# Two-layer mLSTM and neighbourhood-attention backbone on one core: finished mLSTM tiles transposed one projection later, a weight subtraction on GpSimd, and an end spread over four projections

## The chip, the cores and the metric

The kernel runs on one core of a Trainium2 chip. The metric is device time in microseconds (us) of one execution. A core has a matmul engine (TensorE, PE in the profile; its weight loads are PEld), three engines for elementwise work (VectorE or DVE, ScalarE or ACT, GpSimd or POOL), and SyncE (SP), which here issues the transfers (DMAs) between memory and the core. Each engine works through its own instructions in order; semaphores make one wait for another. Matmuls accumulate in PSUM banks, all other tiles lie in SBUF.

## The reference

Two layers on 1024 latent tokens and 256 context tokens of width 1024. In each layer one projection feeds two head groups, an mLSTM (a matrix memory, run in both directions over chunks of tokens) with 8 heads, and neighbourhood attention with 8 heads; their outputs are projected together, and a squared-ReLU MLP follows. Cut to the part in question:

```python
def step(carry, xs):                     # mlstm_scan, one chunk of tokens
    C, n, m = carry
    ...
    s = jnp.einsum('bhtd,bhsd->bhts', qc, kc) * w_intra
    num = w_prev[..., None] * jnp.einsum('bhtd,bhde->bhte', qc, C) + jnp.einsum('bhts,bhse->bhte', s, vc)
    qn = w_prev * jnp.einsum('bhtd,bhd->bht', qc, n) + jnp.sum(s, axis=-1)
    h = num / jnp.maximum(jnp.abs(qn), jnp.exp(-m_t))[..., None]
    ...
    C = w_c[..., None, None] * C + jnp.einsum('bhs,bhsd,bhse->bhde', w_s, kc, vc)
...
y = (head_layernorm(hx_f + hx_b, norm_g) * jax.nn.sigmoid(o.astype(f32))).astype(q.dtype)
...
y_m, yc_m = mlstm_group(qm, km, vm, om, gm, qmc, kmc, vmc, omc, gmc, b_gate, norm_g, cos, sin, need_ctx)
y_n, yc_n = neighborhood_attention(qn, kn, vn, qnc, knc, vnc, rpb, rows, need_ctx)
y = jnp.concatenate([y_m, y_n], axis=-1)
x = x + g1 * (y @ w_out[l])
```

In the last layer the mLSTM and attention outputs of the context tokens are not needed.

## The kernel before

Every large matmul is made of three (L94 to L96, `mm3`): each operand is split into a high part in a reduced format and a low part, and high times high, high times low and low times high are added up in one bank. For weights, `split_chunk` (from L74) loads a chunk of 128x1024 into one of two buffers `wraw`; ACT casts it to `whi` (L88), and DVE subtracts to get `wlo` (L89). There are four such pairs. For the chunks of the mLSTM projection `less_last` (L82) first subtracts, inside each head, the last value column from the other 63.

The mLSTM stage (`mlstm_kv`, then `mlstm_out`) goes over four pairs of heads (`pr`) and, inside a pair, over five slots `i` of 256 tokens. `project_j` makes a slot's projection: two banks of 24 matmuls each, 512 columns wide, or 256 in slots without an output tile (the context slot of the last layer). Four chunks of weights belong to a pair, so a new set is split at each pair boundary. Keys and values taken from a projection at pair `pr` are those of the next pair. A slot with an output gives a tile: queries `qr`, the output gate `og` (ACT, then a product on POOL, L657), and a decay table `w` that a DMA broadcasts (`w<-gscr`, L644) and DVE (L662) and ACT (L663) turn into weights.

Behind a projection stands a `gap`, which does three steps of the pipeline, for three different tiles:

- for the newest tile: transposes of the queries (L573), scores and the state's part (L673, L674), and on DVE the scores weighed (L682) and the state's part scaled (L691);
- for the tile before it: values (L699, out of bank by ACT as `nt`, L702), transposes back (L708), and the norm on DVE (`mlstm_norm`, L714 to L737), which divides, normalizes and multiplies by the gate, into a tile `hs` (two buffers, its constant column set by POOL, L723);
- for the tile before that: two transposes of `hs` (`mlstm_turn`, L747), ACT's copy `yT` (L750), and a store to memory (L752).

A gap also makes the transposes of new keys (L504) and the state updates: DVE scales values into `vw` (L521), PE multiplies them with the keys (L532), and DVE adds up the states (L539, L546). At the start of the stage this is done for all five slots of the first pair in one go, ten L521 and forty L532, with six `vw` buffers.

At the end of the stage the queries and keys of attention are begun: `qk_project(W, gi, ...)` for three groups of tokens `gi` (context 256, then 512 and 512), keys first. `mlstm_out` makes the three key projections, with the last two gaps between them, and `na_qk` then evicts the keys (L800 on ACT, L801 on DVE), makes the query projections and evicts them (L813, L814 on ACT, L816 on DVE). In attention L955 and L965 are the scores.

Pools with a number of buffers and a scheduler that fixes the order of each engine's instructions before the run decide where an instruction stands; `behind()` holds PE work behind the PE instruction that was written last. L158 and L183 belong to the opening (the modulation by `c`), L209 is a piece of the modulation of later steps that DVE does in between.

The lines that set the end of `mlstm_out` (L627 to L638):

```python
with self.behind():
    keys.append(self.qk_project(Wq[0], 0, hi, lo))
gap(due[len(seq)])
with self.behind():
    keys.append(self.qk_project(Wq[0], 1, hi, lo))
gap([])
keys.append(self.qk_project(Wq[0], 2, hi, lo, "q"))
self.mlstm_turn(l)
return Wq, keys
```

Of the kernel before, what the change touches and what calls it, by code (L numbers as in the profile page):

```python
# [11 lines left out]
F32 = mybir.dt.float32  # L12
# [11 lines left out]
HD = 64  # L24
# [23 lines left out]
class Kern:  # L48
# [30 lines left out]
    def less_last(self, raw, n, c):  # L79

        v = raw[:, :n].rearrange("p (k c) -> p k c", c=c)[:, :, 128:256].rearrange("p k (h e) -> p k h e", e=HD)
        self.nc.vector.tensor_sub(v[:, :, :, 0:HD - 1], v[:, :, :, 0:HD - 1], v[:, :, :, HD - 1:HD].to_broadcast([128, n // c, 2, HD - 1]))  # L82

    def split_raw(self, raw, n):
        nc = self.nc
# [424 lines left out]
    def kv_weigh(self, pr, i):  # L510
# [7 lines left out]
        for u in range(2):  # L518
            vw = self.mp.tile([128, 256], F32, name="vw", bufs=WV)[:].rearrange("p (s h e) -> p s h e", s=2, h=2)
            ws = tab[:, 2 * i + u, 1, :, pr * 2:pr * 2 + 2].unsqueeze(3).to_broadcast([128, 2, 2, 64])  # L520
# [36 lines left out]
    def mlstm_out(self, l, hi, lo, need_ctx, W):  # L557

        n2, skip = NT // 2, 0 if need_ctx else 1
        seq = [(pr, i) for pr in range(4) for i in range(n2)]  # L560
        groups = [[(pr, i) for i in range(o, min(o + GROUP, n2))] for pr in range(4) for o in range(skip, n2, GROUP)]
        due = {seq.index(g[-1]) + 1: g for g in groups}
        self.scored, self.turning, states, tiles = [], [], [], {}
        Wq, keys = [], []

        def gap(group):

            now = [tiles.pop(t) for t in group]
            with self.behind():
                p = self.bank() if now or states else None  # L570
                for z, t in enumerate(now):
                    for u in range(2):
                        self.nc.tensor.transpose(p[:, (2 * z + u) * 128:(2 * z + u + 1) * 128], t["qr"][:, u, :], self.ident)  # L573
                spare = 2 - len(now)
                held = [self.kv_turn(*s, p[:, (len(now) + z) * 256:(len(now) + z + 1) * 256]) for z, s in enumerate(states[:spare])]
                if now:
                    n = len(now) * 256
                    qT = self.mb.tile([128, 256 * GROUP], F32, name="qT", bufs=2)
                    self.nc.scalar.mul(qT[:, :n], p[:, :n], 0.125)
                    for z, t in enumerate(now):  # L580
                        t["qT"] = qT[:, z * 256:(z + 1) * 256].rearrange("p (u t) -> p u t", u=2)
                for f in held:
                    f()
                for s in states[spare:]:
                    self.kv_turn(*s)
                self.mlstm_turn(l)
            with self.behind():
                for s in states:
                    self.kv_state(*s)
                    if s[1] == n2 - 1:  # L590
                        self.kv_back(s[0])
                states.clear()
                for t in self.scored:
                    self.mlstm_values(t)
            with self.behind():
                for t in now:
                    self.mlstm_scores(t)
            with self.behind():
                for t in self.scored:
                    self.mlstm_back(t)  # L600
            for t in now:
                self.mlstm_weigh(t)
            for t in self.scored:
                self.mlstm_norm(t)
            for t in now:
                self.mlstm_before(t)
            self.scored = now
            self.tick(True)

        for n, (pr, i) in enumerate(seq):  # L610
# [3 lines left out]
            with self.behind():  # L614
                accs = self.project_j(W, i, hi, lo, 512 if mine else 256)
# [10 lines left out]
            if pr < 3:  # L626
                self.kv_weigh(pr + 1, i)  # L627
                states.append((pr + 1, i))
        Wq.extend(self.qk_weights(l, 0, which) for which in (1, 0))
        with self.behind():  # L630
            keys.append(self.qk_project(Wq[0], 0, hi, lo))
        gap(due[len(seq)])
        with self.behind():
            keys.append(self.qk_project(Wq[0], 1, hi, lo))
        gap([])
        keys.append(self.qk_project(Wq[0], 2, hi, lo, "q"))
        self.mlstm_turn(l)
        return Wq, keys  # L638

    def mlstm_tile(self, l, pr, i, acc):  # L640
        nc, mp = self.nc, self.mb
        tab = self.gt[0]
        w = mp.tile([128, 2, 2, 256], F32, name="w", bufs=GB)
        nc.sync.dma_start(w[:].rearrange("p s h t -> p (s h) t"),  # L644
# [65 lines left out]
    def mlstm_norm(self, t):  # L710

        nc, mp, tab, i, pr, hh = self.nc, self.mb, self.gt[0], t["i"], t["pr"], t["hh"]
# [6 lines left out]
        nc.vector.tensor_tensor(den[:], den[:], tab[:, 2 * i:2 * i + 2, 3, :, pr * 2:pr * 2 + 2], ALU.max)  # L719
        nc.vector.reciprocal(d8, d8)  # L720
        nc.vector.tensor_tensor(h8[:, :, 0:63], h8[:, :, 0:63], d8.unsqueeze(2).to_broadcast([128, 8, 63]), ALU.mult)
        hs = mp.tile([128, 2, 2, 64], F32, name="hs", bufs=2)
        nc.gpsimd.memset(hs[:, :, :, 63:64], 0.0)  # L723
        nc.vector.tensor_add(hs[:, :, :, 0:63], hh[:, :, 0, :, 0:63], hh[:, :, 1, :, 0:63])
        hs4 = hs[:].rearrange("p u h e -> p (u h) e")
# [9 lines left out]
            nc.vector.tensor_scalar(hs4[:, z, :], hs4[:, z, :], mv[:, z, 0:1], rs[:, z:z + 1], ALU.subtract, ALU.mult)  # L735
        hsf = hs[:].rearrange("p u h e -> p u (h e)")
        nc.vector.tensor_mul(hsf, hsf, t["og"][:])  # L737
        self.turning.append((pr, i, hsf))

    def mlstm_turn(self, l):  # L740

# [41 lines left out]
    def na_qk(self, l, pr, hi, lo, need_ctx, W=(), accs=()):  # L783
# [6 lines left out]
        for which in (1, 0):  # L790
            wh, wl = W[1 - which] if W else self.qk_weights(l, pr, which)
            for gi, (g0, n) in enumerate(GROUPS):
                if which == 0 and gi == 0 and not need_ctx:
                    continue
                acc = accs[gi] if which == 1 and gi < len(accs) else self.qk_project((wh, wl), gi, hi, lo)
                for h in range(2):
                    a, b = slice(h * 64, h * 64 + 64), slice(64 - h * 64, 128 - h * 64)
                    if which == 1:
# [1050 lines left out]
WRAW = 2  # L1849
VB = 10  # L1850
TB = 7
WV = 6
GROUP = 1
GB = 4
OB = 5
QB = 3
CONSTS = {"cT": 16, "ident": 128, "fg": 8, "n1g0": 8, "n2g0": 8, "n1g1": 8, "n2g1": 8, "bada0": 48, "bada1": 48, "bgate0": 2, "bgate1": 2}
# [120 lines left out]
```

## Time and profile before

| | |
|---|---|
| median of 3 runs | 2904.61 us (2904.39 to 2906.29) |
| the profiled execution | 2902.07 us |
| its span, first to last instruction | 2900.3 us |
| mean granted PE clock | 0.992 |
| busy: PE, DVE, ACT, POOL | 97%, 76%, 44%, 2% |
| the mLSTM stage's `mlstm_out`, layer 0 | about 125 to 456 us |
| the same, layer 1 | about 1681 to 1970 us |

A row of the timeline gives start and duration in us, engine, line, operation, out<-in, the tile's shape, and in brackets the idle time of that engine before it and what ended it. Rows of groups give count, busy time and mean in ns, and behind the bar the idle time before them. "PE q L747 <- DVE hs L737: 20.4, 8, 5.6" says that PE's L747 waited for DVE's L737 for 20.4 us in all, 8 times, 5.6 at most. Durations in a timeline overlap a little, since matmuls are pipelined; the distance between two starts is the better measure there.

### The profile page before, as it was taken

To read this page: it belongs to the slowest core of one execution; us is meant where nothing else is said; L and a number is where in the kernel's file an instruction comes from. 1 tells how busy PE (TensorE), PEld (TensorE's weight loads), DVE (VectorE), ACT (ScalarE), POOL (GpSimd) and SP (SyncE) were. 2 spreads that over 40 slices of the span, in tenths; PEclk is the share of its full clock that TensorE was granted. 3 is DMA by queue.
4 is the path that set the end of the run, shared out by engine and by line. 5 is a ranking of instruction groups with operands and counts; after the bars stand their busy time and mean duration, and the time that the engine had idled before them with its cause. 6 is when DMAs were issued, how large, how long until landed. Compare 5 with 4: busy or idle time off the path is not lost.

```text
span 2900.3 us, 45396 instructions
## 1 busy us (share of the span) xinstructions
PE 2825.2 (97%) x16500; PEld 2383.2 (82%) x16500; DVE 2205.7 (76%) x4947; ACT 1267.6 (44%) x2472; POOL 70.4 (2%) x153
## 2 busy tenths in 40 slices
PE   8999999999999999999999999999999999999998
PEld 5877778888888888888889987778887788888888
DVE  7779977776798777589877778767775887769774
ACT  5333334564553333344554333325564533334443
POOL 0000000010000000000000000000010000000000
PEclk9999999999999999999999999999999999999999
DMA  7434422236446555798977222223346354478672
GB/s 247 134 122 138 150 77 87 91 114 203 149 156 237 192 196 199 271 322 287 322 256 251 69 77 77 73 67 109 113 137 196 128 177 152 156 246 311 218 250 101
DMA packets 279264, 497.40 MB, mean 171 GB/s; under 512 B 23648, under 2 KB 119904, under 8 KB 279040
## 3 DMA queue, kind: packets, MB, share of 16 engines
q1 hardware_dynamic: 279040, 494.50, 51.1%
q8 instruction: 130, 2.13, 0.3%
q14 instruction: 94, 0.77, 0.1%
HBM read 398.82 MB, written 95.59 MB: 170 GB/s over the span
## 4 chain that ended last, share of the span: by engine, by line
PE 73%; DVE 12%; issue 6%; DMA 5%; ACT 2%; SPq 1%; DVEq 0%; POOL 0%; ACTq 0%; POOLq 0%
PE q L94 13%; PE q L96 13%; PE q L95 13%; PE mm L94 9%; PE mm L95 9%; PE mm L96 9%; PE q L1017 1%; DVE wlo L89 1%; PE q L699 1%; DMA raw<-hid 1%; DMA S<-rpbt 1%; PE q L673 1%; DMA w<-gscr 1%; PE q L965 1%; PE q L983 1%
## 5 line engine op out<-in xcount | busy, mean ns | idle before, releaser
L94 PE MATMUL q<-ah,whi 128*128 128x512 f32 (+1 forms) x1472 | 550.5, 374 | 3.1 <-ACT ah L1067 2.4
L96 PE MATMUL q<-ah,wlo 128*128 128x512 f32 (+1 forms) x1472 | 548.1, 372 | 0.7 <-DVE wlo L1068 0.5
L95 PE MATMUL q<-al,whi 128*128 128x512 f32 (+1 forms) x1472 | 548.7, 373 | 0.0
L94 PE MATMUL mm<-ah,whi 128*128 128x512 f32 (+1 forms) x1120 | 387.3, 346 | 1.5 <-ACT whi L88 1.2
L96 PE MATMUL mm<-ah,wlo 128*128 128x512 f32 (+1 forms) x1120 | 385.3, 344 | 0.5 <-DVE wlo L89 0.5
L95 PE MATMUL mm<-al,whi 128*128 128x512 f32 (+1 forms) x1120 | 385.5, 344 | 0.0
L94 PEld LDWEIGHTS q<-ah,whi 128*128 128x128 f32 x1472 | 278.1, 189 | 52.3 <-ACT ah L1067 3.4
L96 PEld LDWEIGHTS q<-ah,wlo 128*128 128x128 f32 x1472 | 277.8, 189 | 50.8 <-DVE wlo L1068 1.8
L95 PEld LDWEIGHTS q<-al,whi 128*128 128x128 f32 x1472 | 278.3, 189 | 49.1 <-issue 1.4
L94 PE MATMUL mm<-whi,ah 128*128 128x512 f32 (+2 forms) x864 | 311.6, 362 | 1.6 <-ACT whi L88 1.1
L95 PE MATMUL mm<-wlo,ah 128*128 128x512 f32 (+2 forms) x864 | 308.6, 358 | 3.0 <-DVE wlo L89 2.7
L96 PE MATMUL mm<-whi,al 128*128 128x512 f32 (+2 forms) x864 | 308.0, 357 | 0.0
L94 PEld LDWEIGHTS mm<-ah,whi 128*128 128x128 f32 x1120 | 212.4, 190 | 29.0 <-issue 2.0
L96 PEld LDWEIGHTS mm<-ah,wlo 128*128 128x128 f32 x1120 | 212.5, 190 | 26.2 <-DVE wlo L89 1.0
L95 PEld LDWEIGHTS mm<-al,whi 128*128 128x128 f32 x1120 | 212.6, 190 | 25.2 <-issue 0.2
L1067 ACT CAST ah<-raw 128x512 fp32r<-128x512 f32 (+1 forms) x264 | 142.9, 566 | 121.9 <-PE q L96 58.4
L95 PEld LDWEIGHTS mm<-wlo,ah 128*128 128x128 f32 x864 | 164.9, 191 | 26.8 <-DVE wlo L89 5.1
L94 PEld LDWEIGHTS mm<-whi,ah 128*128 128x128 f32 x864 | 164.3, 191 | 26.6 <-ACT whi L88 2.4
L96 PEld LDWEIGHTS mm<-whi,al 128*128 128x128 f32 x864 | 164.6, 191 | 22.8
L1068 DVE TENSOR_TENSOR al<-raw,ah 128x512 fp32r<-128x512 f32 (+1 forms) x264 | 158.0, 622 | 26.9 <-ACT ah L1067 26.7
L1068 DVE TENSOR_TENSOR wlo<-raw,whi 128x1024 fp32r<-128x1024 f32 x84 | 102.6, 1223 | 69.8 <-ACT whi L1067 67.3
L94 PE MATMUL q<-th,whi 128*128 128x512 f32 x384 | 150.3, 391 | 2.1 <-DVE s L1232 2.0
(292 smaller groups left out, 5216.1 us busy)
## 6 DMA issues: line engine op xcount, KB each, us to landing
raw<-w SPq DMA_DIRECT2D x168, 512.0 KB
raw<-hid SPq DMA_DIRECT2D x104, 512.0 KB
wada<-w_adaT SPq DMA_DIRECT2D x96, 512.0 KB
wraw<-w SPq DMA_DIRECT2D x80, 512.0 KB
hid<-hb SPq DMA_DIRECT2D x128, 256.0 KB
hid<-ht SPq DMA_DIRECT2D x96, 256.0 KB
w<-gscr SPq DMA_DIRECT2D x36, 512.0 KB
wada<-w_ada SPq DMA_DIRECT2D x32, 512.0 KB
```

Of the source, the lines that this page charges most:

```text
L89: nc.vector.tensor_sub(lo[:, :n], raw[:, :n], fview(hi[:, :n]))
L94: mm(out, lh, rh, start=start, stop=False, skip_group_check=True)
L95: mm(out, lh, rl, start=False, stop=False, skip_group_check=True)
L96: mm(out, ll, rh, start=False, stop=stop, skip_group_check=True)
L673: mm(t["S"][h][:, o:o + 128], st["kT"][i][hp, u, :], t["qT"][hp, u, :], start=True, stop=True, skip_group_check=True)
L699: self.nc.tensor.matmul(p[h * 64:(h + 1) * 64, u * 256:(u + 1) * 256].rearrange("p (s t) -> p s t", s=2), va[:, u, h, :], t["w"][:, :, h, ...
L965: mm(sl[:, :nl].rearrange("p (r w) -> p r w", w=Rw[1]), q[2 * h + z], krhs[h], start=z == 0, stop=z == 1)
L983: nc.tensor.transpose(tp[:, (h * 2 + a) * 128:(h * 2 + a + 1) * 128], Pn[h][:, a * 128:(a + 1) * 128], self.ident)
L1017: self.nc.tensor.matmul(yp[h * 64:(h + 1) * 64, :], v[h], pt[h], start=i == 0, stop=i == len(tiles) - 1, skip_group_check=True)
L1067: ins = self.nc.scalar.copy(hi, src)
L1068: self.nc.vector.tensor_sub(lo, src, fview(hi))
```

## The change

Four things. `less_last` runs on GpSimd. A normalized tile is put on a list `normal` first and moves to `turning` at the end of the next gap's transposes, so that it is transposed one gap later than before, with three `hs` buffers. The end of `mlstm_out` makes four projections, named by `(which, gi)` with 1 for keys and 0 for queries, and the last steps of the pipeline stand between them one by one; the query projection (0, 1) is among them and is left out of `na_qk`. And there are ten `vw` buffers instead of six, and three `w` buffers instead of four.

```diff
     def less_last(self, raw, n, c):
...
-        self.nc.vector.tensor_sub(v[:, :, :, 0:HD - 1], v[:, :, :, 0:HD - 1], v[:, :, :, HD - 1:HD].to_broadcast([128, n // c, 2, HD - 1]))
+        self.nc.gpsimd.tensor_sub(v[:, :, :, 0:HD - 1], v[:, :, :, 0:HD - 1], v[:, :, :, HD - 1:HD].to_broadcast([128, n // c, 2, HD - 1]))
...
-        self.scored, self.turning, states, tiles = [], [], [], {}
-        Wq, keys = [], []
+        self.scored, self.turning, self.normal, states, tiles = [], [], [], [], {}
+        Wq, keys = [], {}
...
                 self.mlstm_turn(l)
+                self.turning, self.normal = self.normal, []
...
+        def project(which, gi, tag="mm"):
+
+            with self.behind():
+                keys[which, gi] = self.qk_project(Wq[1 - which], gi, hi, lo, tag)
+
+        project(1, 0)
+        gap(due[len(seq)])
+        project(1, 1)
         with self.behind():
-            keys.append(self.qk_project(Wq[0], 0, hi, lo))
-        gap(due[len(seq)])
+            self.mlstm_turn(l)
+            for t in self.scored:
+                self.mlstm_values(t)
+        project(1, 2, "q")
+        self.turning, self.normal = self.normal, []
         with self.behind():
-            keys.append(self.qk_project(Wq[0], 1, hi, lo))
-        gap([])
-        keys.append(self.qk_project(Wq[0], 2, hi, lo, "q"))
+            for t in self.scored:
+                self.mlstm_back(t)
+            self.mlstm_turn(l)
+        for t in self.scored:
+            self.mlstm_norm(t)
+        project(0, 1, "q")
+        self.turning = self.normal
         self.mlstm_turn(l)
         return Wq, keys
...
-        hs = mp.tile([128, 2, 2, 64], F32, name="hs", bufs=2)
+        hs = mp.tile([128, 2, 2, 64], F32, name="hs", bufs=3)
...
-        self.turning.append((pr, i, hsf))
+        self.normal.append((pr, i, hsf))
...
-                acc = accs[gi] if which == 1 and gi < len(accs) else self.qk_project((wh, wl), gi, hi, lo)
+                acc = accs[which, gi] if (which, gi) in accs else self.qk_project((wh, wl), gi, hi, lo)
...
-WV = 6
+WV = 10
...
-GB = 4
+GB = 3
```

The changed file has 17 more lines from L628 on, so that a line of `mlstm_norm` or `mlstm_turn` has a number 17 higher there: L747 is L764, L737 is L754, L699 is L716, L955 is L972, L662 is L679, and the L708 of DVE in the new order is the L691 of before. The scheduler's order moves with the change. Three places, with the name of the semaphore's engine where an instruction waits.

PE at the end of layer 1's mLSTM, where attention begins. Before, nine of the matmuls of the next pair's key projection (L94 to L96) stand between the last query projection and the first scores (L955):

```order
L94 MATMUL mm<-ah_14589,whi 128x512 [waits DVE_49]
L95 MATMUL mm<-al_14597,whi 128x512
L96 MATMUL mm<-ah_14589,wlo 128x512
L94 MATMUL mm<-ah_14590,whi 128x512
L95 MATMUL mm<-al_14598,whi 128x512
L96 MATMUL mm<-ah_14590,wlo 128x512
L94 MATMUL mm<-ah_14591,whi 128x512
L95 MATMUL mm<-al_14599,whi 128x512
L96 MATMUL mm<-ah_14591,wlo 128x512
L955 MATMUL q<-nk_20651,nq 128x256 [waits DVE_49]
```

Now, from the end of the query projection (0, 1) on:

```order
L96 MATMUL q<-ah_15279,wlo 128x512
L764 MATMUL q<-consts,hs 128x128 [waits DVE_49,PE_49,Pool_49]
L764 MATMUL q<-consts,hs 128x128
L94 MATMUL mm<-ah_14589,whi 128x512 [waits DVE_49]
L95 MATMUL mm<-al_14597,whi 128x512
L96 MATMUL mm<-ah_14589,wlo 128x512
L94 MATMUL mm<-ah_14590,whi 128x512
L972 MATMUL q<-nk_20676,nq 128x256 [waits DVE_49]
```

The last transposes of `hs` have moved from ahead of the projection (0, 1) to behind it, and four matmuls are left between them and the first scores.

DVE at the second pair boundary of layer 0, where `wlo` of the first two weight chunks is made (L89), before:

```order
L521 TENSOR_TENSOR vw<-va,tab 128x256 [waits Pool_49]
L89 TENSOR_TENSOR wlo<-wraw,whi 128x1024 [waits Activation_49]
L447 TENSOR_TENSOR ropea<-mm,cos 128x128 [waits PE_49]
L447 TENSOR_TENSOR ropeb<-mm,sin 128x128
L89 TENSOR_TENSOR wlo<-wraw,whi 128x1024 [waits Activation_49]
L450 TENSOR_TENSOR kt<-ropea,ropeb 128x4x32 [waits DVE_49]
```

Now the first chunk stands where it stood, and the second here, behind the next tile's norm has begun (L731 to L738):

```order
L735 SCALAR_TENSOR_TENSOR den<-hh 128x8 [waits DVE_49]
L708 TENSOR_TENSOR hh<-q,tab 128x4x64
L736 TENSOR_TENSOR den<-den,tab 128x8 [waits DVE_49]
L209 ISA wada,mod<-wada,consts 128x1024 [waits DMAHW7_49]
L209 ISA mod 128x1
L737 RECIPROCAL den<-den 128x8 [waits DVE_49]
L89 TENSOR_TENSOR wlo<-wraw,whi 128x1024
L738 TENSOR_TENSOR hh<-hh,den 128x8x63 [waits DVE_49]
L89 TENSOR_TENSOR wlo<-wraw,whi 128x1024 [waits DMAHW0_49,Activation_49]
```

The second chunk's subtraction has moved behind a piece of modulation (L209), and the third chunk's follows it; the fourth chunk's stands behind the end of the norm.

DVE at the start of layer 0's mLSTM stage, where the values of the first pair are scaled (L521), before:

```order
L521 TENSOR_TENSOR vw<-va,tab 128x256 x3
L521 TENSOR_TENSOR vw<-va,tab 128x256 [waits DVE_49]
L521 TENSOR_TENSOR vw<-va,tab 128x256
L662 SCALAR_TENSOR_TENSOR w<-w,tab,mask 128x128 [waits DMAHW7_49,DMAHW6_49]
L662 SCALAR_TENSOR_TENSOR w<-w,tab,mask 128x128 x2
L89 TENSOR_TENSOR wlo<-wraw,whi 128x1024 [waits Activation_49]
L662 SCALAR_TENSOR_TENSOR w<-w,tab,mask 128x128 x2
L521 TENSOR_TENSOR vw<-va,tab 128x256 [waits PE_49]
L89 TENSOR_TENSOR wlo<-wraw,whi 128x1024 [waits Activation_49]
```

Now:

```order
L521 TENSOR_TENSOR vw<-va,tab 128x256 x3
L521 TENSOR_TENSOR vw<-va,tab 128x256 [waits DVE_49]
L521 TENSOR_TENSOR vw<-va,tab 128x256 x3
L521 TENSOR_TENSOR vw<-va,tab 128x256 [waits DVE_49]
L521 TENSOR_TENSOR vw<-va,tab 128x256
L679 SCALAR_TENSOR_TENSOR w<-w,tab,mask 128x128 [waits DMAHW7_49,DMAHW6_49,Activation_49]
```

The last four of the ten stood behind L662, whose data a DMA brings, and waited for PE to give a buffer back; now all ten stand ahead of it.

## The prediction

> **What bounds the kernel now.** I read the page first, then the list of PE's waits, and then the timeline around each wait that stands near a changed line. The page's busy times, and PE's waits (engine, line, what it waited for: us in total, times, longest):
>
> ```profile
> PE 2825.2 (97%) x16500; PEld 2383.2 (82%) x16500; DVE 2205.7 (76%) x4947; ACT 1267.6 (44%) x2472; POOL 70.4 (2%) x153
> PE q L747 <- DVE hs L737: 20.4, 8, 5.6
> PE q L532 <- DVE vw L521: 4.7, 4, 1.3
> ```
>
> PE is busy for 97% of the span of 2900.3 us. Only what shortens PE's idle time, or the stretches in which it runs slowly, can shorten the run. The largest single wait is the one the change is aimed at, L747, the transposes of a finished tile `hs`. All sums below are made against the profiled execution, 2902.07 us; the median of the runs shown is 2904.61, 2.5 higher, and I add 2.5 at the end.
>
> **Term 1, the end of layer 0's mLSTM.** PE's timeline there (start, duration, instruction, and the idle time before it with its releaser), then the same L699 group elsewhere, and the first matmul and the transposes on both sides of a 24-matmul projection:
>
> ```profile
> 433.99 0.66 PE L747 MATMUL q<-consts,hs 128*128 128x128 f32 x2 [5.61 <-DVE hs L737]
> 434.58 1.98 PE L699 MATMUL q<-w,va 128*64 128x256 f32 x8
> 445.67 0.41 PE L747 MATMUL q<-consts,hs 128*128 128x128 f32 x2 [1.27 <-DVE hs L737]
> 447.78 0.92 PE L708 MATMUL q<-consts,nt 128*128 128x128 f32 x4 [0.69 <-ACT nt L702]
> 448.35 0.78 PE L94 MATMUL q<-ah,whi 128*128 128x512 f32 x1
> 455.35 0.38 PE L747 MATMUL q<-consts,hs 128*128 128x128 f32 x2
> 1745.88 1.03 PE L699 MATMUL q<-w,va 128*64 128x256 f32 x8
> ```
>
> Three waits, 5.61 + 1.27 + 0.69 = 7.6 us, go: the first two because the transposed tile is one a projection older, the third because a projection now stands between values and L708. Around them PE is slow: eight L699 take 1.98 against 1.03, and the projection from 448.35 to 455.35 takes 7.00, against 5.74 for the same 24 at 275.39 to 281.13 (below). With the neighbours (L747 0.66 against 0.41 at 445.67, and for the scores right behind, slowed alike, an estimated 0.6) that is 1.8 us at the first place, and with L708 (0.92 against 0.65 at 1963.09) 1.5 at the second. Removed: 10.9 us.
>
> Put back: the third tile's norm has only the projection (0,1), 24 matmuls, 5.5 us, between its L708 and its transposes. DVE's norm chain, first and last instruction, and the weight split that follows it before:
>
> ```profile
> 448.74 0.69 DVE L714 TENSOR_TENSOR hh<-hh,q 128x512 f32<-128x512 f32 x1 [3.21 <-PE q L708]
> 453.94 0.42 DVE L737 TENSOR_TENSOR hs<-hs,og 128x256 f32<-128x256 f32 x1
> 456.40 1.23 DVE L89 TENSOR_TENSOR wlo<-wraw,whi 128x1024 fp32r<-128x1024 f32 x1 [2.03 <-ACT whi L88]
> ```
>
> The chain is 448.74 to 454.36, 5.6 us; in the new order this L89 stands inside it, so 6.85 against 5.5: a new wait of 1.3. These are also the last transposes before attention. Layer 0 still has the projection (0,0) of 256 columns and eight matmuls as cover there, by 5.74 for 24 some 2.9 + 1.9 = 4.8 us, against about 6.2 until the first `nqc` pair is there (worked out in term 2, with shorter copies): 1.4 to 1.5. Net **+8.1**; bounds 5 (both new waits doubled) and 10.9.
>
> **Term 2, the end of layer 1.**
>
> ```profile
> 1949.09 0.66 PE L747 MATMUL q<-consts,hs 128*128 128x128 f32 x2 [5.61 <-DVE hs L737]
> 1960.98 0.41 PE L747 MATMUL q<-consts,hs 128*128 128x128 f32 x2 [1.28 <-DVE hs L737]
> 1963.09 0.65 PE L708 MATMUL q<-consts,nt 128*128 128x128 f32 x4 [0.69 <-ACT nt L702]
> 1969.56 0.41 PE L747 MATMUL q<-consts,hs 128*128 128x128 f32 x2 [0.34 <-DVE hs L737]
> 1970.01 0.37 ACT L750 COPY yT<-q 128x256 f32<-128x256 f32 x1
> 1973.96 0.69 DVE L801 SCALAR_TENSOR_TENSOR nk<-q,nk 64x512 fp32r<-64x512 f32 x1
> 1976.69 1.40 DVE L816 TENSOR_TENSOR nq<-q,nq 64x512 fp32r<-64x512 f32 x2 [2.04 <-ACT nq L814]
> ```
>
> Removed here: 5.61 + 1.28 + 0.69 + 0.34 = 7.9, and 1.8 of slow PE as in layer 0: 9.7. But today the projection (0,1) runs after the last transposes and hides the evictions of the keys (ACT and DVE, from yT at 1970.01 to the end of the last L801 at 1974.65, 4.6 us). In the new order it runs before them; behind the last transposes stand four matmuls (0.9 us), which themselves wait for a bank, and then the scores. The first `nq` pair is ready 4.6 us of keys, about 0.5 for a `nq` copy that now stands between them on ACT, and 1.4 of L816 later, 6.5 after the transposes, so PE idles about 5.6. With the wait of 1.3 for the norm and 1.5 for slow matmuls after it (the value of layer 0, where idle times of 1.27 and 0.69 were enough soon after a long one), 8.4 to 8.8 is given back. Net **+1**; bounds -2 and +5.
>
> [...]
>
> **Term 3, the pair boundaries of layer 1.**
>
> ```profile
> 1745.05 0.41 PE L747 MATMUL q<-consts,hs 128*128 128x128 f32 x2 [1.60 <-DVE hs L737]
> 1814.12 0.41 PE L747 MATMUL q<-consts,hs 128*128 128x128 f32 x2 [1.60 <-DVE hs L737]
> 1883.43 0.41 PE L747 MATMUL q<-consts,hs 128*128 128x128 f32 x2 [3.11 <-DVE hs L737]
> ```
>
> In layer 1 the first slot of a pair has no tile, so only one short projection lies between norm and transposes. Delayed by a gap, the tile is ready: 6.3 us. What is late next is `nt` behind ACT's queue, as at 1963.09 (0.69), once: **+5.7**, bounds 3 (half of it only moves to the next wait on DVE) and 6.3.
>
> **Term 4, ten `vw` buffers.** The state matmuls at the start of both mLSTM stages, grouped (busy, mean ns, idle before): layer 0 from 119 to 126, layer 1 from 1669 to 1676, and eight of them in mid-stage, where the next group begins 0.49 later:
>
> ```profile
> L532 PE MATMUL q<-vw,kt 128*64 128x128 f32 x40 | 3.7, 330 | 2.3 <-DVE vw L521 2.3
> L532 PE MATMUL q<-vw,kt 128*64 128x128 f32 x40 | 3.1, 285 | 2.5 <-DVE vw L521 2.5
> 1745.39 0.66 PE L532 MATMUL q<-vw,kt 128*64 128x128 f32 x8
> ```
>
> Forty need 40 x 0.061 = 2.5 us; they span 5.9 and 5.5. In the new order all ten L521 stand ahead of L662 and its DMA wait, so no L532 waits. Gain 3.4 + 3.0; **+6.5** with 0.1 for what follows, bounds 4.8 (the waits alone) and 7.1.
>
> **Term 5, the weight subtraction on GpSimd, and the order around it.** DVE's L82 and the nearest POOL work, by groups, and one POOL instance:
>
> ```profile
> L82 DVE TENSOR_TENSOR wraw<-wraw 128x252 f32<-128x252 f32 (+1 forms) x30 | 12.5, 429 | 0.8 <-DMA wraw<-w_j 0.7
> L657 POOL TENSOR_TENSOR og<-og,mng 128x256 f32<-128x256 f32 x36 | 28.4, 788 | 198.7 <-ACT og L656 183.0 <-PE q L532 15.6
> 274.35 1.10 POOL L657 TENSOR_TENSOR og<-og,mng 128x256 f32<-128x256 f32 x1 [1.72 <-ACT og L656]
> ```
>
> DVE is freed of 12.5 us, hidden behind PE in most places; one L82 costs about 0.8 on POOL (up to 1.1, as the row at 274.35) instead of 0.43, on an engine with 70 us of work; there it stands among the `og` products, which wait for ACT, so a late `og` holds a chunk up (1.72 of idling ahead of that row), and nothing else queues behind it. [...]
>
> What counts is the order. At the second pair boundary of layer 0:
>
> ```profile
> 270.71 1.22 DVE L89 TENSOR_TENSOR wlo<-wraw,whi 128x1024 fp32r<-128x1024 f32 x1
> 272.25 1.22 DVE L89 TENSOR_TENSOR wlo<-wraw,whi 128x1024 fp32r<-128x1024 f32 x1
> 273.93 0.38 SPq L74 DMA_DIRECT2D wraw<-w_j  x1
> 275.39 0.48 PE L94 MATMUL mm<-whi,ah 128*128 128x512 f32 x1
> 277.61 1.28 DVE L209 CUSTOM_DVE_ANT_0 wada<-wada,consts 128x1024 f32<-128x1024 f32 x1
> 281.37 0.73 PE L94 MATMUL mm<-whi,ah 128*128 128x512 f32 x2 [0.24 <-ACT whi L88]
> 282.79 0.50 PE L95 MATMUL mm<-wlo,ah 128*128 128x512 f32 x1 [0.69 <-DVE wlo L89]
> 348.42 0.33 SPq L74 DMA_DIRECT2D wraw<-w_j  x1
> 350.41 0.38 SPq L74 DMA_DIRECT2D wraw<-w_j  x1
> 352.62 1.05 ACT L88 CAST whi<-wraw 128x1024 fp32r<-128x1024 f32 x1 [1.40 <-DMA wraw<-w_j]
> 357.16 1.04 ACT L88 CAST whi<-wraw 128x1024 fp32r<-128x1024 f32 x1 [3.49 <-DMA wraw<-w_j]
> ```
>
> Chunk 1's L89 moves from 272.25 to behind L209, that is to about 279.05, ready 280.3. PE wants it 14 matmuls after 275.39, at 278.6: 1.7. It also frees the raw buffer of chunk 3, whose transfer leaves at 280.3 instead of 273.93; of two later transfers one took from 348.42 to 352.62, 4.2 us, the next, behind others, from 350.41 to 357.16, 6.7; alone as it is here I take 4.2. Landed 284.5, POOL 0.8, L88 1.05, L89 1.2: 287.6, wanted at 285.7: 1.9. So 3.7 with small change, against 0.93 now: -2.8. At the third boundary no L209 stands there, and the same sum gives an estimated 0.8; I take it as even with today: 0 to +0.4. In layer 1 the pairs of L89 move closer together: +0.7, bounds 0 and 1.7. The first two L82 leave DVE's queue in the opening, where PE waits for DVE: +0.4, bounds -0.5 and 1.3. Term 5 together: **-1.4** (-2.8 + 0.3 + 0.7 + 0.4), bounds -9 (6.4 at the second boundary, as in rival 3, and half of it at the third) and +2.
>
> Three `w` buffers: the transfer of tile n leaves a slot later, and L662 with it, but its first user on DVE (L682) still comes two gaps, some 30 us, later; cost 0, hidden behind two slots of projections, and if a transfer ever took longer than those, that slot would wait for the rest. The third `hs` buffer keeps the norm from waiting for the delayed transposes; without it the next norm would stand behind PE. The delayed transposes take ACT's copy `yT` and its store on SP with them by one slot; the stores stay in the same order, and only the output projection reads them.
>
> **Sum**: 8.1 + 1.0 + 5.7 + 6.5 - 1.4 = 19.9. 2902.07 - 19.9 = 2882.2, and 2.5 for the median: **2884.5 us**.
>
> **Rivals.**
> 1. The waits re-form. DVE is busy for 76% and is the releaser of all four terms; with the tile's wait gone, PE would wait in the same gaps for weighed scores or `nt`, and the openings of attention give more back. Terms 1 to 3 at their low bounds, 5 - 2 + 3 = 6 instead of 14.8, with terms 4 and 5 as above: 2893.3. For it speaks that 0.69 stands right behind 1.27 in both layers; against it that L699 itself shows no wait in any gap.
> 2. The change does not do what it says: PE arrives earlier at loads that come no earlier, at the attention opening and at the weight chunks, and gets nothing but the 5 us that term 4's waits are worth: 2900. Against it: the L747 waits name DVE, not a transfer.
> 3. Slower: the chain raw transfer, L82 on POOL, L88, L89, next transfer over two raw buffers becomes the bound at all six pair boundaries. With POOL at 1.10 and the late chunk 6.7 us on its way, chunk 3 comes 4.7 late after the 1.7 of chunk 1; 6.4 - 0.9 = 5.5 each, 33 in all, against gains of 21.3: 2916. It decides from 3.6 us a boundary. Against it: the new order shows the late L89 at two boundaries, and the L209 that makes it harmful at one.
>
> **Chances.** Forecast (2878 to 2890) 0.62, rival 1 0.22, rival 2 0.10, rival 3 0.06. Faster by over 0.2% (5.8 us, about what a measurement of this kernel can tell from no change), under 2898.8: the forecast and nearly all of rival 1, 0.83; within 0.2%: 0.11; slower 0.06. The range 2873 to 2901 leaves out rival 3 and part of rival 2; its low end is the upper bounds of terms 1 to 5, 31 us.
>
> **What would show it.** Right: no transposes of `hs` waiting 5.6 in either layer, only 1.3 at the last of each; no L532 waits; L972 of layer 1 waiting for `nq` some 5 us; one boundary of layer 0 with L95 waiting 1.5 to 2 for L89, twice. Wrong: waits on `nt` or weighed scores in place of the old ones, or waits of over 3 us on L88 and L89 at every pair boundary.

## The result, and the profile after

| | before | changed |
|---|---|---|
| median of the runs, us | 2904.50 (4 runs, 2900.70 to 2906.29) | 2877.73 (4 runs, 2876.22 to 2880.97) |
| profiled execution | 2902.07 | 2878.26 |
| its span | 2900.3 | 2876.5 |

The ratio is 0.9911, with a 95% interval of 0.9894 to 0.9928: 26.8 us faster by the medians, 23.8 by the two profiled executions. The forecast was 2884.5, 19.9 us less than the profiled execution of before.

From the page after the change PE's and POOL's busy times, the group of the moved subtraction (count, busy, mean ns), and from the list of PE's waits (total, times, longest) those that answer to the ones shown of before:

```profile
PE 2814.8 (98%) x16500; PEld 2379.2 (83%) x16500; DVE 2197.0 (76%) x4917; ACT 1265.7 (44%) x2472; POOL 95.4 (3%) x183
L82 POOL TENSOR_TENSOR wraw<-wraw 128x252 f32<-128x252 f32 (+1 forms) x30 | 25.8, 859 | 850.4 <-DMA raw<-hid 669.2 <-DMA wraw<-w_j 99.0 <-DMA wraw<-w_kvg 36.8
PE q L764 <- DVE hs L754: 2.3, 2, 1.1
PE mm L94 <- DVE nk L818: 3.0, 1, 3.0
PE mm L95 <- DVE wlo L89: 3.0, 4, 1.6
PE q L725 <- ACT nt L719: 1.5, 2, 1.0
```

The waits for a finished tile fell from 20.4 us in eight places to 2.3 in two, and the waits for `vw` are gone. PE is busy for 10.4 us less with the same 16500 matmuls, in part since fewer of them run slowly (the mean granted clock is 0.994, before 0.992). Where the time went is read best from the distance between the two traces at the same point of the program. In the table below, each row is such a point: the start of a PE instruction in the changed kernel's trace minus its start in that of before, and in the last columns the same for the changed kernel profiled once more (`e8_changed_again`) and for two of the experiments below. "Gap" is the first transpose of queries in the gap of that pair and slot.

| point | changed | again | e1_delay_only | e6_one_more_ahead |
|---|---|---|---|---|
| first L532 of layer 0 | +0.06 | -0.15 | +0.16 | +0.03 |
| first gap of layer 0 | -4.25 | -4.47 | +0.10 | -4.29 |
| gap ahead of layer 0's second pair boundary | -3.66 | -4.25 | -0.04 | -3.92 |
| gap behind it | -1.28 | -2.19 | -0.05 | -1.81 |
| last gap of layer 0 | -2.60 | -3.48 | -1.17 | -3.12 |
| end of layer 0's attention | -10.54 | -11.89 | -11.07 | -14.03 |
| first L532 of layer 1 | -7.50 | -11.86 | -9.85 | -13.81 |
| first gap of layer 1 | -9.68 | -14.71 | -7.21 | -16.08 |
| last gap of layer 1 | -19.04 | -23.84 | -12.80 | -25.55 |
| end of layer 1's attention | -22.79 | -29.18 | -20.69 | -34.29 |
| last projection | -23.81 | -31.04 | -20.25 | -36.54 |

A single trace carries some microseconds of its own between these points: the changed kernel's second profile is 7.2 us shorter than its first. The largest piece, 3.0 us, lies between the end of layer 0's attention and the start of layer 1, and most of that at one instruction, a projection of the MLP that waits for a loaded tile (the changed kernel, and the changed kernel again):

```profile
1221.76 0.77 PE L94 MATMUL q<-ah,whi 128*128 128x512 f32 x2 [4.40 <-ACT ah L1084]
1217.51 0.73 PE L94 MATMUL q<-ah,whi 128*128 128x512 f32 x2 [2.17 <-ACT ah L1084]
```

In the trace of before this wait is 2.44. The first trace of the changed kernel loses 3.0 us between the layers and the second next to nothing, so this loss goes with the execution and not with the change. The gap between the traces' 23.8 and the medians' 26.8 is another matter: the profiled execution of before lies 2.4 under its median, and that of the changed kernel 0.5 above its own.

The end of layer 0's mLSTM on PE, in the changed kernel:

```profile
434.12 0.38 PE L764 MATMUL q<-consts,hs 128*128 128x128 f32 x2
434.43 1.08 PE L716 MATMUL q<-w,va 128*64 128x256 f32 x8
441.47 0.38 PE L764 MATMUL q<-consts,hs 128*128 128x128 f32 x2
448.45 0.41 PE L764 MATMUL q<-consts,hs 128*128 128x128 f32 x2 [1.15 <-DVE hs L754]
455.08 0.47 PE L972 MATMUL q<-nk,nqc 128*128 128x256 f32 x2 [1.12 <-ACT nq L831]
```

No tile is waited for but the last (1.15), eight values matmuls take 1.08 instead of 1.98, and attention opens with a wait of 1.12. The end of layer 1, with DVE's first evictions of queries:

```profile
1947.12 0.41 PE L764 MATMUL q<-consts,hs 128*128 128x128 f32 x2 [1.15 <-DVE hs L754]
1950.52 0.80 PE L94 MATMUL mm<-ah,whi 128*128 128x512 f32 x1 [2.99 <-DVE nk L818]
1952.16 1.40 DVE L833 TENSOR_TENSOR nq<-q,nq 64x512 fp32r<-64x512 f32 x2
1952.90 0.58 PE L972 MATMUL q<-nk,nq 128*128 128x256 f32 x1 [0.31 <-DVE nq L833]
```

Between the last transposes and the first scores PE idles for 2.99 + 0.31 us, and the four matmuls that stand there take from 1950.52 to about 1952.6. Two stretches of 20 us show the granted clock (the third number from the end; PE's busy time stands first behind the stretch), of before and of the changed kernel:

```profile
425.00:445.00 20.00, 13.79 (x83) 10.68 (x81) 13.96 (x47) 3.63 (x9) 0.11 (x1) 0.83 0.22 76
1940.00:1960.00 20.00, 14.09 (x84) 10.99 (x82) 13.76 (x46) 3.72 (x9) 0.11 (x1) 0.83 0.24 84
```

```profile
425.00:445.00 20.00, 20.00 (x116) 15.87 (x115) 14.69 (x48) 4.49 (x12) 0.11 (x1) 1.00 0.24 79
1940.00:1960.00 20.00, 15.55 (x66) 12.31 (x65) 14.43 (x44) 8.13 (x18) 0.00 (x0) 0.83 0.38 120
```

In layer 0 the slow stretch is gone. In layer 1 the end of the mLSTM now lies before 1948, and the clock of 0.83 belongs to the opening of attention: the slow matmuls have moved there.

### The profile page after: what moved, and what is told of

The parts are those of the page before. It is cut to its first block, busy times and chain, and to the rows that moved or that the text cites. A ratio compares the mean times of both kernels' runs of the same rounds, so it can differ in the third digit from the quotient of the medians.

```text
span 2876.5 us, 45467 instructions
## 1 busy us (share of the span) xinstructions
PE 2814.8 (98%) x16500; PEld 2379.2 (83%) x16500; DVE 2197.0 (76%) x4917; ACT 1265.7 (44%) x2472; POOL 95.4 (3%) x183
## 4 chain that ended last, share of the span: by engine, by line
PE 59%; DVE 5%; DMA 3%; ACT 1%; issue 1%; SPq 1%; DVEq 0%; ACTq 0%
PE q L94 12%; PE q L96 12%; PE q L95 12%; PE mm L94 6%; PE mm L95 6%; PE mm L96 6%; PE q L1034 1%; PE q L982 1%; DVE wlo L89 1%; DMA wada<-w_adaT 1%; PE q L972 1%; DMA wraw<-yscr 0%; PE q L1000 0%; PE q L1011 0%; DMA raw<-hid 0%
## 5 line engine op out<-in xcount | busy, mean ns | idle before, releaser
L94 PE MATMUL q<-ah,whi 128*128 128x512 f32 (+1 forms) x1472 | 549.3, 373 | 4.9 <-ACT ah L1084 4.4
L96 PE MATMUL q<-ah,wlo 128*128 128x512 f32 (+1 forms) x1472 | 547.5, 372 | 0.8 <-DVE wlo L1085 0.5
L94 PE MATMUL mm<-ah,whi 128*128 128x512 f32 (+1 forms) x1120 | 387.9, 346 | 6.0 <-DVE nk L818 3.0
L96 PE MATMUL mm<-ah,wlo 128*128 128x512 f32 (+1 forms) x1120 | 385.9, 345 | 0.5 <-DVE wlo L89 0.5
L94 PEld LDWEIGHTS q<-ah,whi 128*128 128x128 f32 x1472 | 277.4, 189 | 55.0 <-ACT ah L1084 5.2
L96 PEld LDWEIGHTS q<-ah,wlo 128*128 128x128 f32 x1472 | 277.6, 189 | 50.4 <-DVE wlo L1085 1.6
L94 PE MATMUL mm<-whi,ah 128*128 128x512 f32 (+2 forms) x864 | 310.8, 361 | 2.0 <-ACT whi L88 0.8
L96 PE MATMUL mm<-whi,al 128*128 128x512 f32 (+2 forms) x864 | 307.7, 356 | 0.0
L94 PEld LDWEIGHTS mm<-ah,whi 128*128 128x128 f32 x1120 | 212.6, 190 | 34.3 <-DVE nk L818 3.6
L96 PEld LDWEIGHTS mm<-ah,wlo 128*128 128x128 f32 x1120 | 212.7, 190 | 26.1 <-DVE wlo L89 1.0
L94 PEld LDWEIGHTS mm<-whi,ah 128*128 128x128 f32 x864 | 164.0, 190 | 26.6 <-issue 1.8
L96 PEld LDWEIGHTS mm<-whi,al 128*128 128x128 f32 x864 | 164.2, 190 | 22.8
L94 PE MATMUL q<-th,whi 128*128 128x512 f32 x384 | 150.5, 392 | 2.5 <-DVE s L1249 2.4
```

The source lines that it names most:

```text
L94: mm(out, lh, rh, start=start, stop=False, skip_group_check=True)
L96: mm(out, ll, rh, start=False, stop=stop, skip_group_check=True)
```

## The experiments

The theory (A): PE's waits for finished tiles and for `vw` were the cost; the delay and the buffers remove them, each by itself, and the spread end adds openings that PE cannot cover. The rivals: that the spread is a part of the gain (B), and that the losses and gains at the pair boundaries belong to the subtraction on GpSimd (C, D). The first four kernels make one part alone on the kernel before; their runs share 22 runs of the kernel before, median 2904.27 us.

**The delay alone** (`e1_delay_only`).

```diff
-        self.scored, self.turning, states, tiles = [], [], [], {}
+        self.scored, self.turning, self.normal, states, tiles = [], [], [], [], {}
...
                 self.mlstm_turn(l)
+                self.turning, self.normal = self.normal, []
...
         keys.append(self.qk_project(Wq[0], 2, hi, lo, "q"))
         self.mlstm_turn(l)
+        self.turning = self.normal
+        self.mlstm_turn(l)
...
-        hs = mp.tile([128, 2, 2, 64], F32, name="hs", bufs=2)
+        hs = mp.tile([128, 2, 2, 64], F32, name="hs", bufs=3)
...
-        self.turning.append((pr, i, hsf))
+        self.normal.append((pr, i, hsf))
```

> The kernel before with only the delay: a finished tile is transposed one gap later (three hs buffers); the end keeps its three key projections and its two gaps, and the last two tiles are transposed one after the other at its end. Theory A (the waits for hs were the cost, and the delay alone takes them away): the waits of 5.61 and 1.27 go in both layers, with the slow matmuls behind them, about 9.5 in layer 0 and 8.5 in layer 1, and 6.3 at the pair boundaries of layer 1: 22 to 25 us faster, as much as the whole change without the vw buffers. Rival B (the end needs the four projections, else the waits come back as nt and the last hs): 5 to 7 at each end at most, 16 us or less in all.

2881.58 us, ratio 0.9926 (0.9911 to 0.9941): 22.7 faster, as theory A expects. At the end of layer 0 its PE shows these (L711 is the transposes back, L750 those of `hs`):

```profile
437.95 0.66 PE L711 MATMUL q<-consts,nt 128*128 128x128 f32 x4 [1.00 <-ACT nt L705]
444.59 0.41 PE L750 MATMUL q<-consts,hs 128*128 128x128 f32 x2 [0.29 <-DVE hs L740]
```

Waits of 1.00 and 0.29 are all that is left of 5.61, 1.27 and 0.69. From the last gap to the end of attention it gains 9.9 us in layer 0 and 7.9 in layer 1; the changed kernel, with the spread end, gains 8.0 and 3.8 in its first trace and 8.4 and 5.3 in its second.

**The spread end alone** (`e2_spread_only`). The changed kernel's end, without the delay (`mlstm_norm` appends to `turning`), the buffers or GpSimd.

```diff
-                self.turning, self.normal = self.normal, []
...
         project(1, 2, "q")
-        self.turning, self.normal = self.normal, []
...
         project(0, 1, "q")
-        self.turning = self.normal
         self.mlstm_turn(l)
```

> The kernel before with only the end spread over four projections, with the query projection (0,1) made ahead; tiles are transposed as soon as before, no other part of the change. Theory A: the 5.61 stays in both layers, only the 0.69 goes, the last transposes wait 0.3 to 1.2, and attention opens with 1.1 (layer 0) and 3.3 (layer 1) of waiting for keys and queries: 2 to 6 us slower. Rival B: 4 us faster or more.

2912.82 us, ratio 1.0033 (1.0017 to 1.0048): 8.5 slower, more than the 2 to 6 of theory A. Its runs go from 2906.77 to 2921.32, and the profiled one is the slowest of them. Its transposes of `hs` (L761) in the last full gap of each layer:

```profile
435.41 0.66 PE L761 MATMUL q<-consts,hs 128*128 128x128 f32 x2 [5.62 <-DVE hs L751]
1960.58 0.66 PE L761 MATMUL q<-consts,hs 128*128 128x128 f32 x2 [5.62 <-DVE hs L751]
```

The long wait is untouched, and the openings are added. Rival B falls. Where the 2 to 3 us beyond A's range come from was not taken apart.

**The buffers alone** (`e3_buffers_only`).

```diff
-WV = 6
+WV = 10
...
-GB = 4
+GB = 3
```

> The kernel before with only ten vw and three w buffers. Theory A (the terms add up): the state matmuls at the two starts gain 4.3 and 2.1, as in the changed kernel, and since DVE's order now has the second weight chunk of layer 0's second boundary behind L209, about 2.4 is lost there and 0.8 at the first: 3 to 4 us faster. Rival C (that loss belongs to the subtraction on GpSimd): 6 to 6.5 faster, with no loss at the boundaries.

2898.76 us, ratio 0.9981 (0.9972 to 0.9991): 5.5 faster. By the medians that is more than A's 3 to 4 and nearer to C's 6 to 6.5, so the trace has to decide. It has A's parts: at the two starts it gains 4.3 and 1.9, and at the second boundary of layer 0 it loses 2.3, without anything on GpSimd. Rival C falls: that loss comes with the buffers.

**GpSimd alone** (`e4_gpsimd_only`).

```diff
-        self.nc.vector.tensor_sub(v[:, :, :, 0:HD - 1], ...)
+        self.nc.gpsimd.tensor_sub(v[:, :, :, 0:HD - 1], ...)
```

> The kernel before with only the subtraction of less_last on GpSimd. Theory A: within 2 us of the kernel before; the pair boundaries of layer 1 gain at most the weight waits of 0.98 and 0.76. Rival D (the 3 us which the pair boundaries of layer 1 gained beyond their hs waits come from this part): 3 us or more faster. Rival C: 2.5 to 3.5 slower in layer 0.

2907.24 us, ratio 1.0012 (1.0002 to 1.0021): 3.0 slower, on the other side of what D expects and more than the 2 that A allowed, and layer 0 shows nothing of C's loss. But the pair boundaries of layer 1 are not as before. Its waits for `hs` there:

```profile
1745.75 0.41 PE L747 MATMUL q<-consts,hs 128*128 128x128 f32 x2 [3.12 <-DVE hs L737]
1816.60 0.66 PE L747 MATMUL q<-consts,hs 128*128 128x128 f32 x2 [3.13 <-DVE hs L737]
1888.99 0.41 PE L747 MATMUL q<-consts,hs 128*128 128x128 f32 x2 [3.12 <-DVE hs L737]
```

They were 1.60, 1.60 and 3.11, and the waits for `wlo` ahead of them (0.22, 0.76 and 0.76 in the trace of before) are gone. The weight splits now go earlier on DVE, and the norm later. From the first to the last gap of layer 1 this trace loses 5.0 us. With the waits comes a slow clock (0.50), behind two of the three; in the trace of before it stands behind none of them (1.00). The two places where it sets in lie 68.27 us apart here, 20 times 3.41. Counted from them in steps of 3.41 us, for each of the three waits the step with the most of its idle time, and the next one:

```profile
1743.82:1747.23 3.41, 1.48 (x17) 1.12 (x18) 3.41 (x12) 0.98 (x3) 0.95 (x3) 1.00 0.02 10
1747.23:1750.64 3.41, 3.41 (x23) 2.63 (x20) 2.68 (x10) 1.25 (x3) 0.00 (x0) 0.50 0.55 169
1812.09:1815.50 3.41, 1.39 (x12) 1.15 (x11) 3.12 (x18) 1.37 (x6) 0.00 (x0) 1.00 0.68 228
1815.50:1818.91 3.41, 2.31 (x14) 1.68 (x16) 2.52 (x11) 1.47 (x4) 0.14 (x2) 0.50 0.13 41
1887.18:1890.59 3.41, 1.60 (x18) 1.12 (x18) 1.89 (x9) 1.44 (x5) 0.11 (x1) 1.00 0.23 85
1890.59:1894.00 3.41, 3.41 (x31) 2.84 (x28) 3.19 (x11) 0.58 (x1) 0.00 (x0) 1.00 0.56 192
```

PE is busy for 1.48 and 1.39 us of the first two of these steps, and the clock is 0.50 in the next; in the third it is busy for 1.60, and the clock stays at 1.00. The last section comes back to this.

The waits gave theory F: alone this costs, but with the delay the later norm is free and the weight waits stay away.

The four parts make -22.7 + 8.5 - 5.5 + 3.0 = -16.7 us; together they made -26.8. So some 10 us are interaction: the spread and the subtraction cost less, or nothing, once the delay is there. The next four were run on one chip, with a median of 2902.23 for the kernel before.

**The changed kernel with the old end** (`e5_old_end`), **the same with the subtraction on DVE** (`e7_old_end_dve`), and **the changed kernel again** (`e8_changed_again`).

```diff
         project(1, 1)
-        with self.behind():
-            self.mlstm_turn(l)
-            for t in self.scored:
-                self.mlstm_values(t)
+        gap([])
         project(1, 2, "q")
-        self.turning, self.normal = self.normal, []
-        with self.behind():
-            for t in self.scored:
-                self.mlstm_back(t)
-            self.mlstm_turn(l)
-        for t in self.scored:
-            self.mlstm_norm(t)
-        project(0, 1, "q")
+        self.mlstm_turn(l)
         self.turning = self.normal
         self.mlstm_turn(l)
```

> The changed kernel with the end of the kernel before: three key projections, a gap behind each of the first two, the last two tiles transposed together behind the third, and the query projection (0,1) made where it was, behind them. Theory A (with the delay the spread earns nothing and costs its openings): the last transposes still wait at most 1, but the waits of 1.1 and 3.3 at the openings of attention and the 1.15 for the norm go: 4 to 6 us faster than the changed kernel, and 30 faster than before. Rival B (the spread is part of the gain): 3 us or more slower than the changed kernel.

> The kernel of the run with the old end, with the subtraction of less_last back on DVE. Theory F (on GpSimd the subtraction lets the weight splits go ahead of the norm on DVE: the weight waits of PE turn into later norms, which cost 3.0 when a tile is transposed at once, and nothing when it is transposed a gap later): the pair boundaries of layer 1 gain 1.1, 1.3 and 3.2 instead of 3.05, 3.1 and 3.2 against the kernel before, and the second one of layer 0 loses about as much; 3 to 5 us slower than with the subtraction on GpSimd. Rival G (the parts only add up, and by itself the subtraction on GpSimd was 3 us slower): 2 to 3 us faster.

> The changed kernel once more, on the same chip as the three others: 26 to 28 us faster than the kernel before, by both theories.

The changed kernel again: 2875.04 us (2871.04 to 2878.50), ratio 0.9908 (0.9896 to 0.9921). With the old end: 2872.36 (2870.44 to 2873.75), ratio 0.9899 (0.9885 to 0.9912), 2.7 faster; the two ranges overlap, so this is A's direction, with less than its 4 to 6. By the traces, from the last gap to the end of attention, the old end gains 6.8 in layer 1 (9.0 in the run with DVE) against 3.8 and 5.3 with the spread, as A expects. In layer 0 it gains 6.4 (8.6 with DVE) against 8.0 and 8.4: in its trace later waits inside the attention (0.78, 1.05 and 0.38 us on the softmax) and a clock of 0.91 between 660 and 680 us take the gain back. Whether that belongs to the old end or to this execution stays open.

With the subtraction back on DVE: 2872.32 (2870.05 to 2876.08), ratio 0.9900 (0.9887 to 0.9914), equal to the one on GpSimd. Neither F's 3 to 5 nor G's gain is there in the time. At the pair boundaries F holds: the first two of layer 1 gain 1.5 and 1.8 us with DVE and 3.1 and 3.1 with GpSimd, the third 3.3 with both. Those 2.9 us show at their place in the trace, but the whole runs do not tell the two kernels apart.

**One more projection ahead** (`e6_one_more_ahead`, again as `e11_one_more_again`).

```diff
         self.turning = self.normal
         self.mlstm_turn(l)
+        project(0, 2, "q")
         return Wq, keys
```

> The changed kernel with a fifth projection, the queries (0,2), made ahead behind the last transposes and into a bank of the other kind. Theory A (PE waits there because only four matmuls cover the eviction of the keys, and those want a bank that the keys still hold): the wait of 2.99 in layer 1 and the 1.1 in layer 0 go, 3 to 4 us faster than the changed kernel. Rival E (the queries' evictions on ACT and DVE are the bound there, whatever PE does meanwhile): the wait moves to the first scores, no gain.

2865.25 us (2864.78 to 2869.86), ratio 0.9879 (0.9864 to 0.9894): 9.8 faster than the changed kernel on the same chip, with no overlap of the two ranges, and the fastest of all. The waits of 2.99 and 1.12 are gone, and nothing of over 0.25 us stands in their place at the first scores; E falls. The same stretches of its trace:

```profile
425.00:445.00 20.00, 20.00 (x114) 15.79 (x113) 14.59 (x50) 4.41 (x11) 0.10 (x1) 1.00 0.26 87
1940.00:1960.00 20.00, 19.34 (x116) 16.95 (x116) 16.01 (x41) 14.08 (x29) 0.00 (x0) 1.00 0.48 144
```

PE is busy for 19.34 of 20 us at the opening of layer 1 instead of 15.55, and the clock is back to 1.00. The 9.8 us are more than the 3 to 4 expected. From the last gap to the end of attention its trace gains 10.9 us in layer 0 and 8.7 in layer 1, against 8.4 and 5.3 in the second trace of the changed kernel: 5.9 more, by the idle times that went and the clock. The other 4 of the 9.8 us the traces do not place. The second time it took 2868.24 (2865.73 to 2871.21), ratio 0.9888 (0.9873 to 0.9903), beside a median of 2902.78 for the kernel before, which is 34.5 faster, a little less than the 36 to 38 expected:

> The kernel with one more projection ahead, with ten vw and three w buffers, again on the same chip: 36 to 38 us faster than the kernel before, by all theories.

**Which buffers make the loss at the second boundary** (`e9_six_vw_four_w` and `e10_six_vw_three_w`, both with one more projection ahead).

```diff
-WV = 10
-GB = 3
+WV = 6
+GB = 4
```

and six and three.

> The kernel with one more projection ahead, with six vw and four w buffers as before the change. Theory A: the state matmuls lose 4.3 and 2 to 5 again, and the second pair boundary of layer 0 gets back its 2.1 to 2.4 and the first its 0.5 to 0.8: 3 to 6 us slower than the kernel with ten and three.

> The same with six vw and three w buffers. Theory H (it is the third w buffer that moves the second weight chunk's split behind the modulation at layer 0's second boundary, since L662 for a tile now stands one gap later on DVE; the vw buffers have no part in it): the loss of 2.1 to 2.4 at that boundary stays and the gain of the state matmuls is gone, 2.5 to 3.5 us slower than with six and four. Rival I (ten vw buffers crowd DVE there): the boundary is as before the change, equal to six and four.

2870.79 us (2870.66 to 2871.55) and 2871.20 (2869.45 to 2880.97), against 2868.24 with ten and three: by the medians 2.6 and 3.0 slower, and the intervals of all three ratios overlap. The times are not what was expected, 3 to 6 for the first, and for the second 2.5 to 3.5 slower than the first by theory H; they cannot tell H from I. The traces can. The changed kernel at the second boundary of layer 0, and below it the kernel with six `vw` and three `w`:

```profile
276.79 0.50 PE L95 MATMUL mm<-wlo,ah 128*128 128x512 f32 x1 [1.60 <-DVE wlo L89]
282.93 0.73 PE L94 MATMUL mm<-whi,ah 128*128 128x512 f32 x2 [0.84 <-ACT whi L88]
284.19 0.50 PE L95 MATMUL mm<-wlo,ah 128*128 128x512 f32 x1 [0.53 <-DVE wlo L89]
```

```profile
282.77 0.50 PE L95 MATMUL mm<-wlo,ah 128*128 128x512 f32 x1 [1.59 <-DVE wlo L89]
289.14 0.73 PE L94 MATMUL mm<-whi,ah 128*128 128x512 f32 x2 [1.07 <-ACT whi L88]
290.40 0.51 PE L95 MATMUL mm<-wlo,ah 128*128 128x512 f32 x1 [0.53 <-DVE wlo L89]
```

The same three waits stand with six `vw` buffers and with ten; with four `w` buffers there is none of over 0.25 us there for weights, and that boundary runs 1.36 us faster than before the change. So it is having three `w` buffers instead of four that makes the loss, as H says, and I falls. Ten `vw` buffers with four `w` buffers were not tried.

## Why the prediction was right

The time lies 6.8 us below the forecast of 2884.5 and inside its range (its own sum, 2882.2 and 2.5, is 2884.7); the waits of the forecast went, and those it added are the ones in the trace. From the start of layer 0's stage to the end of layer 1's attention, without the stretch between the layers, the trace gains 25.9 us where the terms add up to 19.9, so the forecast was low in its own terms, by terms 2 and 3 above all. That the first trace's 23.8 is nearer to it is luck: this execution lost 3.0 between the layers. By its terms, in the first trace of the changed kernel:

- **Term 1, layer 0's end**, +8.1: 8.0 from the last gap to the end of attention. The new waits were 1.15 and 1.12, forecast 1.3 and 1.4 to 1.5. The delay alone makes 9.9 there.
- **Term 2, layer 1's end**, +1: 3.8, and 5.3 in the second trace. The step that was mis-sized is "PE idles about 5.6": it idled 3.3. It counted the first pair of L833 (1.40) before the first scores, which start after the first of the two (1952.16 to 1952.90), and ACT and DVE finished the keys some 0.4 earlier. That is 1.1 of the difference: the scores start 5.4 after the transposes, not 6.5. The other 1.2 of idle time are no gain, since the four matmuls, taken at 0.9, ran slowly and took 2.1. The slow clock behind it came as forecast: 0.83 in that stretch, 0.91 in the second trace, so the row after the short waits of layer 0 was a good guide here.
- **Term 3, the pair boundaries of layer 1**, +5.7: 9.4 with the +0.7 that term 5 had for them (the shown 6.31 less 0.69 is 5.6, not 5.7). The three `hs` waits are worth 6.3; the rest is the 1.7 us of weight waits that went with the subtraction on GpSimd, and what follows them. The forecast treated the two parts as independent. `e4_gpsimd_only` shows that they are not: without the delay the same weight waits come back as `hs` waits, 3.12 instead of 1.60.
- **Term 4, ten `vw`**, +6.5: 4.3 and 2.2, forecast 3.4 and 3.0, and no L532 waits. In layer 0 a slow stretch went with the waits: from 115 to 135 us the granted clock is 0.91 in the trace of before and 1.00 in that of the changed kernel.

The group of forty L532 at the start of layer 0 in the changed kernel, to be held against 3.7 us busy and 2.3 idle before:

```profile
L532 PE MATMUL q<-vw,kt 128*64 128x128 f32 x40 | 2.4, 275 | 0.0
```

- **Term 5**, -1.4. The size at the second boundary was right, 2.4 lost against 2.8 forecast, with 1.60 for chunk 1 (1.7 forecast) and 1.37 for chunk 3 (1.9). Its cause was not: the forecast put it under the subtraction on GpSimd, and "three `w` buffers ... cost 0" is the step that fails. With three `w` buffers, and not with four, DVE's order has the second weight split behind L209. That it is L679, standing later on DVE, which pushes the split there is argued and not shown. The first boundary lost 0.8 more, where a wait of 1.0 for `nt` stands; with the buffers alone that wait is 0.35 and the loss 0.6. The third gained 1.0 where 0 to 0.4 was forecast. L82 took 0.86 on POOL, forecast 0.8; nothing in the opening came of it.

Rival 1, waits that re-form as `nt`, is hardly there: PE waits 1.5 us for `nt` in two places, and before it was 1.9 in three; only the wait of 1.0 at the first boundary of layer 0 is new. Rival 2 is seen only as scatter, in the wait of 2.2 to 4.4 for a load between the layers. Rival 3 would have needed 3.6 us at all six boundaries; it was 2.4 at one. The trial of its mechanism was `e4_gpsimd_only`, the only part besides the spread that was slower by itself.

## What to carry to other kernels

Where an engine in order waits for the result of a chain on another, give the consumer one more stage of distance before rearranging the work between them: here the delay by itself gained 22.7 us where the whole change gained 26.8, and it also made another edit harmless that cost 3 us without it. When a projection is moved ahead to cover one wait, look for what it covered at its old place; one more projection there was worth some 7 to 10 us. A smaller buffer can cost time without any wait of its own, by the order that the scheduler makes of it, so parts are to be tried alone and together.

## What the runs showed of the hardware that was not expected

Idle times well short of the 5.61 us at the end of layer 0 were enough for the slow clock, but not every time. At layer 1's opening, idle times of 1.15 and 2.99 us with only the two transposes of 0.4 us between them left a granted clock of 0.83 over 20 us in one trace of the changed kernel and 0.91 in the other, and with the 2.99 and 0.31 covered it was 1.00. A single wait with no other near it could do the same. There are four such waits for `hs` in layer 1, of 3.11 to 3.13 us, in the kernel before (one) and in `e4_gpsimd_only` (three); two of them were followed by a clock of 0.50 and two by none.

The traces show where these differ. Between 150 and 2800 us the traces of before and of the changed kernel have 12 slow stretches, of 3.41 or 6.83 us each, and in each trace all points at which the clock changes there lie a multiple of 3.41 us apart. Counted in these steps, as for `e4_gpsimd_only` above, the step with the most idle time of the wait in the kernel before (3.11, ended at 1883.43), and the next one:

```profile
1881.64:1885.05 3.41, 1.62 (x18) 1.12 (x18) 1.89 (x9) 1.44 (x5) 0.11 (x1) 1.00 0.26 91
1885.05:1888.46 3.41, 3.41 (x31) 2.85 (x28) 3.19 (x11) 0.59 (x1) 0.00 (x0) 1.00 0.60 189
```

PE is idle for 1.79 us of the first. For the two waits with a slow clock behind them the rows give 1.93 and 2.02 us, for the two without 1.79 and 1.81. Over all steps between 150 and 2800 us that began at full clock, 1539 in the traces of before and of the changed kernel, the next step was slow in nine of nine with 2.00 to 3.02 us of idle time, in three of 13 with 1.26 to 1.79, and in none of 1517 with 1.22 or less. So of these four waits of about the same length, the two with more of it in one step were followed by a slow stretch and the two with less were not; a trace without a slow stretch does not show that such a wait is harmless.

Two profiles of the changed kernel differed by 7.2 us, with 2.2 of that at a single wait for a load, so a difference of a few microseconds between two traces is to be looked for at its place and not in the total.
